# Ten transposes taken from the matrix engine: 32x32 blocks on VectorE, and a trip through HBM between partitions

## The chip, the cores and the metric

The kernel runs on one core of a Trainium2 chip. The metric is device time in microseconds; 446.53 us is the median of three runs before the change. The core's engines run side by side, each with its own queue of instructions in a fixed order: TensorE (PE, matrix products and the transposes), VectorE (DVE), ScalarE (ACT), GpSimd (POOL) and SyncE (SP, which here only issues weight transfers).

## What is computed

Two decoder layers over 256 tokens of width 1024. What matters here is the first layer, in which four retention heads and eight latent-attention heads (worked as four pairs) run from one input projection into one output projection:

```python
h = x @ w_in
rq, rk, rv, rg, mq, mkv, mkr, mg = _split(h, EVEN_SPLITS)
q_r = retnet_rotate(_heads(rq, RET_HEADS), pos)
k_r = retnet_rotate(_heads(rk, RET_HEADS), pos)
o_r = head_group_norm(retention_chunkwise(q_r, k_r, _heads(rv, RET_HEADS)))
ret_out = (_merge(o_r) * jax.nn.silu(rg.astype(jnp.float32))).astype(x.dtype)
...
o_m = causal_attention(q_full, k_full, v_m, (MLA_NOPE + MLA_ROPE) ** -0.5)   # softmax over keys, times v
mla_out = (_merge(o_m) * jax.nn.silu(mg)).astype(x.dtype)
return jnp.concatenate([ret_out, mla_out], axis=-1) @ w_out
...
x = layer_norm(DN_ALPHA * x + y, ln_g[i], ln_b[i])
```

The second layer (`moba_layer`, 16 heads of causal attention with rotary q and k, gate and output projection) is not touched.

## The kernel before

Every fp32 product is made of three float32r products (`mm3`, L174 to L176): each operand is split into a high part (ACT, L179) and a remainder (DVE, L180). So each weight tile `raw` that SP fetches becomes `w_h` on ACT and `w_l` on DVE, in six buffers each (`WBUFS`), and PE works through them unit by unit; a unit is one 512 KB weight tile. Within a head or pair the projections are units named by their PSUM tiles: `pq`/`pkk` (queries and keys of a retention head), `pv`, `pg` (values, gate), `pmg`, `pn`, `pvv` (gate, the two up-projections of a pair).

PE's order is written out by hand. Between the units, `tick()` lets waiting generators go one step; the tables at the head of the file say how many units each step waits. `retention` adds `scores` (PSUM tile `pst`, then `sd` and its split `sT`), `values` (`po`, normalised into `ro`; POOL computes the reciprocal root `rstd`) and `merge` (`ro` times the gate, then `transposed`). `mla` adds `attend` (scores `sc`, `softmax` into `prob`, `prob_T`, then the product `pom`). The order on DVE, ACT and POOL is set by the scheduler, once, when the program is built: each engine takes its instructions in that order, and one that waits holds up those behind it.

Two places transpose on PE. `transposed` turns the gated head output `ro` (two token halves of 128x512) into the layout that the output projection needs, in eight 128x128 transposes per head, and splits what lands in PSUM into `rT_h`, `rT_l`. `prob_T` turns the six 128x128 blocks of a pair's probabilities into `pT_h`, `pT_l`. The eight transposes of the rotary queries `qr` (`rotary_queries`) share two buffers, tag `ro`, with the head outputs.

Of the kernel before, what the change touches and what calls it, by code (L numbers as in the profile page):

```python
# [9 lines left out]
F32 = mybir.dt.float32  # L10
F32R = mybir.dt.float32r
# [6 lines left out]
P = 128  # L18
S = 256
NT = S // P  # L20
# [11 lines left out]
WBUFS = 6  # L32
TAIL = 5
HOLD = 5
SCO = 6, 4, 5, 8
CPT = 3, 3, 4, 5
MRG = 1, 2, 2, 6
CSC = 3, 3, 3, 3
CAV = 4, 4, 4, 1
MSC = 2, 2, 2, 2  # L40
MPT = 5, 4, 3, 3
MAV = 3, 1, 3, 3
VAL = 1, 2, 1, 1
LAT1, LAT2, QR = 5, 2, 7
WARM = 8
BY_DVE = 1
CSK = 6
DECK = 7

OFF = np.cumsum([0, 1024, 1024, 2048, 2048, 256, 256, 64, 1024])  # L50
# [107 lines left out]
def trunk(ctx, tc, x, lng, lnb, w, cst, dec, out):  # L158
    nc = tc.nc
    cp = ctx.enter_context(tc.tile_pool(name="const", bufs=1))  # L160
    wp = ctx.enter_context(tc.tile_pool(name="weights", bufs=1))
    even = ctx.enter_context(ExitStack())
    wk = even.enter_context(tc.tile_pool(name="even", bufs=1))
    ps = ctx.enter_context(tc.tile_pool(name="psum", bufs=1, space=bass.MemoryType.PSUM))
# [194 lines left out]
    def transposed(srcs, n, hi, lo):  # L359

        for d in range(0, n, 2):
# [4 lines left out]
                    nc.tensor.transpose(pv[:, k, t * P:(t + 1) * P], srcs[t][:, (d + k) * P:(d + k + 1) * P], ident)  # L366
            split_to(hi[:, d:d + 2, :], lo[:, d:d + 2, :], pv)

    lat = []
    got_qpe = []  # L370

# [91 lines left out]
    def retention(h, mid=None):  # L463

        pq, pkk = pp("pq"), pp("pkk")
        v4 = [z.rearrange("p (c s) -> p c s", c=2) for z in (pq, pkk)]
        for _ in range(KD // 2):
            ks, wv = load("qk")
            for i, k in enumerate(ks):
                for c in range(4):  # L470
                    mm3(v4[c // 2][:, c % 2, :], wv, x_rows(k), lambda z: z[:, i, c * P:(c + 1) * P],
                        lambda z: z, start=k == 0 and c % 2 == 0, stop=k == KD - 1)
            tick()
        qkT = []
        both = [wk.tile([P, 4, S], F32R, name="rqk_" + e, tag="rqk_" + e) for e in "hl"]
        for n, p in enumerate(v4):
            a = wk.tile([P, 2, S], F32, name="rot_a", tag="rot_a")
            b = wk.tile([P, 2, S], F32, name="rot_b", tag="rot_b")
            nc.vector.tensor_tensor(a, p, cosr[:, None, :].to_broadcast([P, 2, S]), op=OP.mult)
            nc.vector.tensor_tensor(b, p, sinr, op=OP.mult)  # L480
            nc.vector.tensor_tensor(a, a, b[:, ::-1, :], op=OP.add)
            qkT.append([z[:, 2 * n:2 * n + 2, :] for z in both])
            split_to(*qkT[n], a)
        qT, kT = qkT
        got = {}

        def scores():
            pst = at("pst")
            for c in range(2):
                mm3(pst[:, :S], kT, qT, lambda z: z[:, c, :P], lambda z: z[:, c, :], start=c == 0, stop=c == 1)  # L490
            for c in range(2):
                mm3(pst[:, S:S + P], kT, qT, lambda z: z[:, c, P:], lambda z: z[:, c, P:], stop=c == 1)
            sd = wk.tile([P, S + P], F32, name="sd", tag="sd")
            nc.vector.tensor_tensor(sd[:, :S], pst[:, :S], decay[:, h, :], op=OP.mult)
            nc.vector.tensor_tensor(sd[:, S:], pst[:, S:S + P], decay[:, h, :P], op=OP.mult)
            got["sT"] = split(sd, [P, S + P], "sT")
            yield 1

        def values():
            while "v" not in got or "sT" not in got:  # L500
                yield 0
            sT, v = got["sT"], got["v"]
            po = [at("po") for t in range(NT)]
            mm3(po[0], sT, v[0], lambda z: z[:, :P], lambda z: z, start=True, stop=True)
            mm3(po[1], sT, v[0], lambda z: z[:, P:S], lambda z: z, start=True)
            mm3(po[1], sT, v[1], lambda z: z[:, S:], lambda z: z, stop=True)
            got["o"] = []
            for t in range(NT):
                st = wk.tile([P, 6], F32, name="st", tag="st", bufs=2)
                nc.vector.bn_stats(st, po[t])  # L510
                r = rstd_of(st, LN_EPS, True)
                o = wk.tile([P, RDV], F32, name="ro", tag="ro", bufs=2)
                state["late"] = nc.scalar.activation(o, po[t], AF.Identity, scale=r[:, 0:1], bias=r[:, 1:2])
                got["o"].append(o)
            yield 1

        def merge():
            while "o" not in got:
                yield 0
            for t in range(NT):  # L520
                nc.vector.tensor_tensor(got["o"][t], got["o"][t], got["g"][t], op=OP.mult)
            yield MRG[h]
            hi = wk.tile([P, 4, S], F32R, name=f"rT{h}_h", tag="rT_h", bufs=2)
            lo = wk.tile([P, 4, S], F32R, name=f"rT{h}_l", tag="rT_l", bufs=2)
            transposed(got["o"], 4, hi, lo)
            for i in range(4):
                catT[4 * h + i] = (hi[:, i, :], lo[:, i, :])
            yield 1

        add(scores(), SCO[h])  # L530
        if mid:
            mid(h)
        pvv = [pp("pv") for t in range(NT)]
        block_proj("v", x_rows, pvv)
        vh = wk.tile([P, NT, RDV], F32R, name="rv_h", tag="rv_h")
        vl = wk.tile([P, NT, RDV], F32R, name="rv_l", tag="rv_l")
        for t in range(NT):
            split_to(vh[:, t, :], vl[:, t, :], pvv[t])
        got["v"] = [(vh[:, t, :], vl[:, t, :]) for t in range(NT)]
        add(values(), VAL[h])  # L540
        pg = [pp("pg") for t in range(NT)]
        block_proj("g", x_rows, pg)
        got["g"] = [gate(pg[t], [P, RDV], "rgate", 2) for t in range(NT)]
        add(merge())
# [40 lines left out]
    def prob_T(prob, j, tag, bufs):  # L585

        pt = at("ppt")
        for b in range(3):
            nc.tensor.transpose(pt[:, b * P:(b + 1) * P], prob[:, j, b * P:(b + 1) * P], ident)
        return split(pt[:, :3 * P], [P, 3 * P], tag, bufs=bufs)  # L590

    def av(o, pT, v, cols, start):

# [28 lines left out]
    def mla(p):  # L622
# [32 lines left out]
        def attend():  # L655
            while not got_qpe:
                yield 0
            sc = [at("sc") for a in range(2)]
            for a in range(2):
                causal_scores(sc[a], [z[:, a, :] for z in qn], [z[:, a, :] for z in kn])  # L660
            paired_scores(sc, [z[:, p, :] for z in qpe], kpe, False)
            prob = softmax(sc, (MN + MR) ** -0.5, "msm", 1)
            yield MPT[p]
            pTs = [prob_T(prob, a, "pT", 2) for a in range(2)]
            yield MAV[p]
            po = at("pom")
            pov = po.rearrange("p (a s) -> p a s", a=2)
            for a in range(2):
                av(pov[:, a, :], pTs[a], v, slice(a * P, (a + 1) * P), start=a == 0)
            og = wk.tile([P, 2, S], F32, name="mog", tag="og")  # L670
            nc.vector.tensor_tensor(og, pov, sg.rearrange("p (a s) -> p a s", a=2), op=OP.mult)
            hi, lo = split(og, [P, 2, S], f"mT{p}", tag="mT", bufs=2)
            for i in range(2):
                catT[16 + 2 * p + i] = (hi[:, i, :], lo[:, i, :])
            yield 1
# [163 lines left out]
    def attend_odd(q, qT, kT, v, got):  # L839

        st = {}

        def first():
            sc = [at("sc") for a in range(4)]
            quad_scores(sc, qT, kT)
            for d in range(2):
                st[d] = softmax(sc[2 * d:2 * d + 2], CD ** -0.5, "csm", 2)

        def second():
            for d in range(2):  # L850
                st[d] = [prob_T(st[d], a, "pT", 4) for a in range(2)]

        def third():
            for d in range(2):
                po = at("poc")
                pov = po.rearrange("p (a s) -> p a s", a=2)
                for a in range(2):
                    c = (q % 2) * S + d * P + a * CD
                    av(pov[:CD, a, :], st[d][a], v, slice(c, c + CD), start=a == 0)
                og = wk.tile([P, S], F32, name="cog", tag="og", bufs=2)  # L860
                for a in range(2):
                    rs = slice(a * CD, (a + 1) * CD)
                    nc.vector.tensor_tensor(og[rs, :], pov[:CD, a, :], got["g"][rs, d * S:(d + 1) * S], op=OP.mult)
                oT[2 * q + d] = split(og, [P, S], f"oT{2 * q + d}")

        first()
        yield CPT[q]
        second()
        yield CAV[q]
        while "g" not in got:  # L870
            yield 0
        third()
        yield 1
# [109 lines left out]
```

## Time and profile before

| | |
|---|---|
| median of 3 runs (446.32 to 446.73) | 446.53 us |
| profiled execution | 446.2 us |
| its span, first to last instruction | 444.4 us |
| busy: PE / DVE / ACT / POOL | 435.2 / 330.1 / 247.7 / 9.8 us |
| granted TensorE clock, mean | 0.995 |

The profiled execution stands 0.3 us under the median; 1.8 us of it lie outside the span. Busy times of several engines overlap, so they don't add up to the span; what counts is which engine the last chain of work runs through.

### The profile page before, as it was taken

Reading aid. Unit: us, or ns where it says so; the run is one execution under the profiler, and the core shown is the slowest. Engines: PE = TensorE matmul, PEld = TensorE weight load, DVE = VectorE, ACT = ScalarE, POOL = GpSimd, SP = SyncE. Lnnn points to the kernel's source line nnn. Section 1 sums busy time; section 2 is a strip of 40 time slices with the busy share of each in tenths; the row PEclk is TensorE's granted clock in tenths of the full one; section 3 lists DMA queues with packets and bytes.
Section 4 is the critical chain, followed back from the end, with each engine's and each line's share of the span. In section 5 each row is a group of like instructions: output and inputs, shape, how many; then the busy total and the mean of one; then the engine's idle time right before and its main releaser. Section 6 shows DMA issues by size and latency. Waiting matters only on the chain.

```text
span 444.4 us, 7652 instructions
## 1 busy us (share of the span) xinstructions
PE 435.2 (98%) x2958; PEld 389.5 (88%) x2958; DVE 330.1 (74%) x587; ACT 247.7 (56%) x438; POOL 9.8 (2%) x18
## 2 busy tenths in 40 slices
PE   8999999999999999999999999999999999999993
PEld 6998899988998888889998888888899999999883
DVE  5899788785876865556498569668767698889747
ACT  6777466653656553345465755503645869596810
POOL 0000000000000000000000000000000000000001
PEclk9999999999999999999999999999999999999998
DMA  8977545454463466454546557812866363634002
GB/s 297 367 228 235 184 143 188 146 170 139 143 196 126 168 215 208 154 190 160 197 143 192 183 185 239 290 50 96 279 194 189 97 191 103 190 96 137 1 1 94
DMA packets 21924, 75.55 MB, mean 170 GB/s; under 512 B 2432, under 2 KB 3072, under 8 KB 21888
## 3 DMA queue, kind: packets, MB, share of 16 engines
q1 hardware_dynamic: 20304, 70.66, 49.8%
q10 hardware_dynamic: 1584, 4.41, 2.7%
q8 instruction: 23, 0.38, 0.3%
q14 instruction: 13, 0.11, 0.1%
HBM read 74.01 MB, written 1.05 MB: 169 GB/s over the span
## 4 chain that ended last, share of the span: by engine, by line
PE 94%; DVE 2%; ACT 2%; issue 1%; DVEq 0%; ACTq 0%
PE pg L174 5%; PE pg L176 5%; PE pg L175 5%; PE pj L174 4%; PE pv L174 3%; PE pj L176 3%; PE pj L175 3%; PE pv L176 3%; PE pv L175 3%; PE acc L174 3%; PE acc L175 3%; PE acc L176 3%; PE pm L307 3%; PE pa L175 3%; PE pa L176 3%; PE pa L174 2%
## 5 line engine op out<-in xcount | busy, mean ns | idle before, releaser
L180 DVE TENSOR_TENSOR w_l<-raw,w_h 128x1024 fp32r<-128x1024 f32 (+3 forms) x133 | 155.8, 1175 | 55.9 <-ACT w_h L179 55.0
L179 ACT ACTIVATE w_h<-raw 128x1024 fp32r<-128x1024 f32 (+3 forms) x133 | 135.2, 1020 | 94.1 <-PE pa L175 19.3
L174 PE MATMUL pj<-xT_hi,w_h 128*128 128x256 f32 x128 | 36.2, 283 | 0.0
L176 PE MATMUL pj<-xT_lo,w_h 128*128 128x256 f32 x128 | 35.8, 279 | 0.0
L175 PE MATMUL pj<-xT_hi,w_l 128*128 128x256 f32 x128 | 35.7, 279 | 0.0
L174 PE MATMUL pg<-w_h,xT_hi 128*128 128x512 f32 x64 | 25.8, 403 | 0.0
L174 PE MATMUL pv<-w_h,xT_hi 128*128 128x512 f32 x64 | 25.6, 400 | 0.0
L175 PE MATMUL pg<-w_h,xT_lo 128*128 128x512 f32 x64 | 25.3, 395 | 0.0
L175 PE MATMUL pv<-w_h,xT_lo 128*128 128x512 f32 x64 | 25.2, 395 | 0.0
L176 PE MATMUL pv<-w_l,xT_hi 128*128 128x512 f32 x64 | 25.2, 395 | 0.0
L176 PE MATMUL pg<-w_l,xT_hi 128*128 128x512 f32 x64 | 25.2, 394 | 0.0
L174 PEld LDWEIGHTS pj<-xT_hi,w_h 128*128 128x128 f32 x128 | 24.0, 187 | 0.4
L175 PEld LDWEIGHTS pj<-xT_hi,w_l 128*128 128x128 f32 x128 | 24.0, 188 | 0.0
L176 PEld LDWEIGHTS pj<-xT_lo,w_h 128*128 128x128 f32 x128 | 24.0, 188 | 0.0
L174 PE MATMUL pq<-xT_hi,w_h 128*128 128x256 f32 x64 | 18.3, 286 | 0.0
L174 PE MATMUL pg<-xT_hi,w_h 128*128 128x256 f32 x64 | 18.1, 283 | 0.0
L174 PE MATMUL pmg<-xT_hi,w_h 128*128 128x256 f32 x64 | 18.0, 282 | 0.0
L174 PE MATMUL pkk<-xT_hi,w_h 128*128 128x256 f32 x64 | 18.0, 281 | 0.0
L175 PE MATMUL pkk<-xT_hi,w_l 128*128 128x256 f32 x64 | 17.9, 280 | 0.0
L175 PE MATMUL pq<-xT_hi,w_l 128*128 128x256 f32 x64 | 17.9, 280 | 0.0
L175 PE MATMUL pmg<-xT_hi,w_l 128*128 128x256 f32 x64 | 17.9, 279 | 0.0
L176 PE MATMUL pmg<-xT_lo,w_h 128*128 128x256 f32 x64 | 17.9, 279 | 0.0
(304 smaller groups left out, 1222.2 us busy)
## 6 DMA issues: line engine op xcount, KB each, us to landing
raw<-w SPq DMA_DIRECT2D x125, 512.0 KB, 4.0
raw<-w SPq DMA_DIRECT2D x7, 416.0 KB, 6.7
raw<-w SPq DMA_DIRECT2D x4, 256.0 KB, 2.7
xn<-x ACTq DMA_DIRECT2D x2, 512.0 KB, 4.4
decay<-dec ACTq DMA_DIRECT2D x1, 512.0 KB, 7.8
decay_ln<-lng ACTq DMA_DIRECT2D x1, 512.0 KB, 4.5
rv_h_ln<-lnb ACTq DMA_DIRECT2D x1, 512.0 KB, 3.9
lng_ln<-lng ACTq DMA_DIRECT2D x1, 512.0 KB, 3.5
```

The source lines that it names most:

```text
L174: nc.tensor.matmul(o, ca(a[0]), cb(b[0]), start=start, stop=False, skip_group_check=True)
L175: nc.tensor.matmul(o, ca(a[1]), cb(b[0]), start=False, stop=False, skip_group_check=True)
L176: state["mm"] = nc.tensor.matmul(o, ca(a[0]), cb(b[1]), start=False, stop=stop, skip_group_check=True)
L179: done = nc.scalar.activation(hi, src, AF.Copy)
L180: nc.vector.tensor_tensor(lo, src, hi.bitcast(F32), op=OP.subtract)
L307: state["mm"] = nc.tensor.matmul(pm[t][j][:, :288], xs[a][:, t * P:(t + 1) * P], wv[b][:, i2 * 288:(i2 + 1) * 288], start=k == 0 and e == ...
```

## The change

For retention heads 0 to 2 and all four pairs, the transposes on PE go. `moved` does the same in three steps: DVE transposes all 32x32 blocks of the tile within their 32 partitions (`turn`); POOL writes the result to HBM (`far`); POOL reads it back in four transfers, one for each group of 32 partitions (`moved`), so that the blocks land on the partitions where they belong. ACT and DVE then split `moved` in SBUF where they split PSUM before. Head 3, the rotary queries, the latents and the second layer keep PE's transposes. The tables of waits get other numbers, and the buffer that GpSimd's transfers use for their descriptors is set to 4096 bytes.

```diff
-SCO = 6, 4, 5, 8
+SCO = 7, 4, 4, 8
...
-MPT = 5, 4, 3, 3
+MPT = 7, 9, 4, 7
...
+MOVE_R, MOVE_M, MOVE_C = 3, 4, 0
...
+    def moved(src, n, w):
+        m = n * P
+        z = wk.tile([P, w], F32, name="turn", tag="turn", bufs=2)[:, :m]
+        nc.vector.transpose(z.rearrange("p (j n q) -> p j n q", j=4, n=n),
+                            src.rearrange("p (n j q) -> p j n q", n=n, j=4))
+        d = wk.tile([P, w], F32, name="moved", tag="moved", bufs=2)[:, :m]
+        far = dram.tile([P, m], F32, name=f"far{m}", tag=f"far{m}", bufs=3)
+        nc.gpsimd.dma_start(far, z)
+        fv = far.rearrange("(i k) (j c) -> j k i c", i=4, j=4)
+        for j in range(4):
+            nc.gpsimd.dma_start(d[j * 32:(j + 1) * 32, :].rearrange("k (i c) -> k i c", i=4), fv[j])
+        return d.rearrange("p (i n q) -> p n i q", i=4, n=n)
...
+            if h < MOVE_R:
+                dst = [moved(got["o"][t], 4, 768) for t in range(NT)]
             yield MRG[h]
...
-            transposed(got["o"], 4, hi, lo)
+            if h < MOVE_R:
+                for t in range(NT):
+                    split_to(*[z[:, :, t * P:(t + 1) * P].rearrange("p n (i q) -> p n i q", i=4) for z in (hi, lo)], dst[t])
+            else:
+                transposed(got["o"], 4, hi, lo)
...
+            if p < MOVE_M:
+                prob = moved_T(prob)
             yield MPT[p]
-            pTs = [prob_T(prob, a, "pT", 2) for a in range(2)]
+            pTs = pair_T(prob, "pT", 2) if p < MOVE_M else [prob_T(prob, a, "pT", 2) for a in range(2)]
...
-    nc = bacc.Bacc("TRN2", target_bir_lowering=False, num_devices=1)
+    nc = bacc.Bacc("TRN2", target_bir_lowering=False, num_devices=1, dynamic_dma_scratch_size=4096)
```

What this does to the order shows at three places. On POOL, from head 0's `rstd` to head 1's, there stood before only the reciprocal roots:

```order
L457 TENSOR_TENSOR rstd_668<-rstd_668,mhalf_75 128x1
L457 TENSOR_TENSOR rstd_678<-rstd_678,mhalf_75 128x1
L457 TENSOR_TENSOR rstd_1252<-rstd_1252,mhalf_75 128x1
L457 TENSOR_TENSOR rstd_1262<-rstd_1262,mhalf_75 128x1
```

Now the transfers of head 0's two token halves (`far512`) and of pair 0 (`far768`) stand between them:

```order
L476 TENSOR_TENSOR rstd_736<-rstd_736,mhalf_77 128x1
L382 DMA far512_778<-turn_775 128x512
L382 DMA far512_787<-turn_784 128x512
L385 DMA moved_777<-far512_778 32x4x128 x4
L385 DMA moved_786<-far512_787 32x4x128 x4
L382 DMA far768_1080<-turn_1077 128x768
L385 DMA moved_1079<-far768_1080 32x4x192 x4
L476 TENSOR_TENSOR rstd_1255<-rstd_1255,mhalf_77 128x1
```

Fifteen transfers came in ahead of head 1's `rstd`, and each group of reads waits for its write to have landed. On DVE, ahead of pair 0's softmax (L558, later L583), there stood before:

```order
L180 TENSOR_TENSOR qpe_l_739<-pt_945,qpe_h_738 128x512
L180 TENSOR_TENSOR qpe_l_739<-pt_952,qpe_h_738 128x512
L180 TENSOR_TENSOR w_l_1184<-raw_1181,w_h_1183 128x1024
L558 ISA neg_1018,msm_m_1016<-sc_989,cs_88 128x128
```

and now:

```order
L183 TENSOR_TENSOR qpe_l_710<-pt_985,qpe_h_709 128x512
L540 TENSOR_TENSOR ro_730<-ro_730,rgate_673 128x512
L498 TENSOR_TENSOR rot_a_1088<-pq_887,cosr_267 128x512
L499 TENSOR_TENSOR rot_b_1089<-pq_887,sinr_268 128x512
L540 TENSOR_TENSOR ro_740<-ro_740,rgate_676 128x512
L183 TENSOR_TENSOR qpe_l_710<-pt_992,qpe_h_709 128x512
L378 STREAM_TRANSPOSE turn_775<-ro_730 128x512
L183 TENSOR_TENSOR w_l_1225<-raw_1222,w_h_1224 128x1024
L500 TENSOR_TENSOR rot_a_1088<-rot_a_1088,rot_b_1089 128x512
L378 STREAM_TRANSPOSE turn_784<-ro_740 128x512
L583 ISA neg_1058,msm_m_1056<-sc_1029,cs_90 128x128
```

Head 0's gating and its two block transposes moved in front of that softmax. On ACT, around the split of head 1's scores (`sT_h`), there stood before:

```order
L179 ACTIVATE w_h_1364<-raw_1362 128x1024
L179 ACTIVATE rv_h_1173<-pv_1084 128x512
L179 ACTIVATE pT_h_1161<-ppt_1157 128x384
L179 ACTIVATE pT_h_1169<-ppt_1165 128x384
L179 ACTIVATE w_h_1399<-raw_1397 128x512
L179 ACTIVATE sT_h_1215<-sd_1212 128x384
```

and now:

```order
L182 ACTIVATE rT0_h_949<-moved_777 128x4x128
L182 ACTIVATE rv_h_1196<-pv_1102 128x512
L182 ACTIVATE w_h_1373<-raw_1371 128x1024
L182 ACTIVATE rv_h_1196<-pv_1103 128x512
L182 ACTIVATE rT0_h_949<-moved_786 128x4x128
L182 ACTIVATE sT_h_1192<-sd_1189 128x384
L182 ACTIVATE w_h_1428<-raw_1426 128x512
L182 ACTIVATE w_h_1449<-raw_1447 128x1024
L182 ACTIVATE pT_h_1289<-moved_1079 128x384
L182 ACTIVATE pT_h_1293<-moved_1079 128x384
```

The splits of head 0's moved halves, which need POOL's transfers, now stand in front of `sT_h`, and pair 0's behind it; the splits on DVE (`rT0_l`, `sT_l`) follow in the same order.

## Rows read from the trace of the kernel before

**Rows 1.** The page: span, busy time, and the chain that ended last.
```profile
span 444.4 us, 7652 instructions
PE 435.2 (98%) x2958; PEld 389.5 (88%) x2958; DVE 330.1 (74%) x587; ACT 247.7 (56%) x438; POOL 9.8 (2%) x18
...
PE 94%; DVE 2%; ACT 2%; issue 1%; DVEq 0%; ACTq 0%
```
**Rows 2.** PE's timeline at head 0's transposes: start, length (us), operation, count.
```profile
62.30 0.28 PE L176 MATMUL pmg<-xT_lo,w_h 128*128 128x256 f32 x1
62.42 1.03 PE L366 MATMUL pt<-cs,ro 128*128 128x128 f32 x8
63.21 0.36 PE L174 MATMUL pmg<-xT_hi,w_h 128*128 128x256 f32 x1
63.41 0.28 PE L175 MATMUL pmg<-xT_hi,w_l 128*128 128x256 f32 x1
```
**Rows 3.** PE's timeline at pair 0's transposes.
```profile
96.08 0.39 PE L176 MATMUL pv<-w_l,xT_hi 128*128 128x512 f32 x1
96.31 0.82 PE L589 MATMUL ppt<-cs,prob 128*128 128x128 f32 x6
96.88 0.48 PE L174 MATMUL pg<-w_h,xT_hi 128*128 128x512 f32 x1
97.19 0.39 PE L175 MATMUL pg<-w_h,xT_lo 128*128 128x512 f32 x1
```
**Rows 4.** Busy time by stretch: PE, PEld, DVE, ACT, POOL, clock, DMA share, GB/s.
```profile
65.00:165.00 100.00, 100.00 (x656) 89.91 (x656) 75.11 (x123) 55.01 (x89) 2.09 (x4) 1.00 0.51 159
165.00:265.00 100.00, 100.00 (x615) 88.11 (x613) 64.28 (x99) 52.24 (x82) 1.04 (x2) 1.00 0.57 181
```
**Rows 5.** DVE's timeline at pair 0's softmax.
```profile
82.29 0.29 DVE L558 CUSTOM_DVE_ANT_0 neg<-sc,cs 128x128 f32<-128x128 f32 x1
...
83.41 0.08 DVE L558 DVE_READ_ACCUMULATOR2_ANT msm_m<- 128x1 f32 x1
84.60 0.69 DVE L479 TENSOR_TENSOR rot_a<-pq,cosr 128x512 f32<-128x512 f32 x1 [1.11 <-PE pq L176]
85.21 0.68 DVE L480 TENSOR_TENSOR rot_b<-pq,sinr 128x512 f32<-128x512 f32 x1
...
86.63 1.19 DVE L180 TENSOR_TENSOR w_l<-raw,w_h 128x1024 fp32r<-128x1024 f32 x1
```
**Rows 6.** PE's timeline: where stages of heads 0 and 1 begin.
```profile
18.53 0.28 PE L174 MATMUL pq<-xT_hi,w_h 128*128 128x256 f32 x1
29.84 0.40 PE L174 MATMUL pv<-w_h,xT_hi 128*128 128x512 f32 x1
79.83 0.22 PE L174 MATMUL sc<-mqk_h 128*128 128x128 f32 x1
82.18 0.38 PE L174 MATMUL pq<-xT_hi,w_h 128*128 128x256 f32 x1
99.75 0.28 PE L174 MATMUL pst<-rqk_h 128*128 128x256 f32 x1
101.09 0.45 PE L174 MATMUL pg<-w_h,xT_hi 128*128 128x512 f32 x1
103.93 0.39 PE L174 MATMUL po<-rv_h,sT_h 128*128 128x512 f32 x1
106.00 0.40 PE L174 MATMUL pg<-w_h,xT_hi 128*128 128x512 f32 x1
```
**Rows 7.** An issue on ACT; POOL's longest group; landing times of transfers.
```profile
251.95 0.33 ACTq L765 DMA_DIRECT2D decay_ln<-lng  x1
...
L750 POOL TENSOR_TENSOR lr<-lr,mhalf 128x1 f32<-128x1 f32 x4 | 3.8, 943 | 174.7 <-DVE lr L742 128.6 <-DVE lr L749 46.1
...
raw<-w SPq DMA_DIRECT2D x4, 256.0 KB, 2.7
...
out<-xn SPq DMA_DIRECT2D x2, 256.0 KB, 2.0
```

More of the change, by code (lines that the diff above doesn't have):

```diff
@@ L34 @@
 HOLD = 5
-SCO = 6, 4, 5, 8
+SCO = 7, 4, 4, 8
 CPT = 3, 3, 4, 5
-MRG = 1, 2, 2, 6
+MRG = 5, 4, 2, 6
 CSC = 3, 3, 3, 3
 CAV = 4, 4, 4, 1
-MSC = 2, 2, 2, 2
-MPT = 5, 4, 3, 3
-MAV = 3, 1, 3, 3
+MSC = 2, 5, 2, 1
+MPT = 7, 9, 4, 7
+MAV = 2, 1, 4, 2
 VAL = 1, 2, 1, 1
-LAT1, LAT2, QR = 5, 2, 7
+LAT1, LAT2, QR = 4, 7, 6
 WARM = 8
@@ L47 @@
 CSK = 6
+MOVE_R, MOVE_M, MOVE_C = 3, 4, 0
+MOVE_ACT = 4
 DECK = 7
@@ L161, in trunk @@
     wp = ctx.enter_context(tc.tile_pool(name="weights", bufs=1))
+    dram = ctx.enter_context(tc.tile_pool(name="dram", bufs=1, space=bass.MemoryType.DRAM))
     even = ctx.enter_context(ExitStack())
@@ L590, in prob_T, with moved_T, pair_T @@
         return split(pt[:, :3 * P], [P, 3 * P], tag, bufs=bufs)
+    def moved_T(prob):
+        return moved(prob.rearrange("p a c -> p (a c)"), 6, 768)
+    def pair_T(d, tag, bufs):
+        res = []
+        for a in range(2):
+            hi, lo = [wk.tile([P, 3 * P], F32R, name=tag + e, tag=tag + e, bufs=bufs) for e in ("_h", "_l")]
+            split_to(*[z.rearrange("p (n i q) -> p n i q", n=3, i=4) for z in (hi, lo)], d[:, 3 * a:3 * a + 3])
+            res.append((hi, lo))
+        return res
     def av(o, pT, v, cols, start):
@@ L847, in first @@
                 st[d] = softmax(sc[2 * d:2 * d + 2], CD ** -0.5, "csm", 2)
+                if q < MOVE_C:
+                    st[d] = moved_T(st[d])
         def second():
             for d in range(2):
-                st[d] = [prob_T(st[d], a, "pT", 4) for a in range(2)]
+                st[d] = pair_T(st[d], "pT", 4) if q < MOVE_C else [prob_T(st[d], a, "pT", 4) for a in range(2)]
         def third():
```

## The prediction

> **What bounds the kernel now.** I read the page first: PE is busy for 98% of the span, and the chain that ended last runs through PE for 94% of it [rows 1]. Next the busy times by stretch: between 65 and 265 us, where all the groups of transposes that go but one lie, PE is busy for 200 of 200 us at full granted clock, DVE for 75 of 100 and then 64 of 100 us, POOL for 2 and 1 us [rows 4]. So in this part every instruction that PE loses is time saved, as long as PE finds no new wait; the other engines have time left over. Then I read PE's timeline around two groups of transposes, for what one costs where it stands, and the starts of PE's stages, to lay the new order out in time.
>
> **What PE loses.** Head 0's eight transposes begin at 62.42; the second matmul after them begins at 63.41. Matmuls of that shape follow each other at 0.12 us (62.30 to 62.42), so without the group it would have begun at 62.54: the group costs 0.87 us [rows 2]. Pair 0's six begin at 96.31, the second matmul after them at 97.19; at 0.23 us from one to the next (96.08 to 96.31) it would have begun at 96.54: 0.65 us [rows 3]. Both give 0.11 us per transpose. Three heads and four pairs: 3 x 0.87 + 4 x 0.65 = **5.2 us**. From the profiled execution's 446.2 us that leaves 441.0; the runs' median stands 0.3 above it, so **441.3 us** if nothing else changes. The odd layer's instructions keep their order (but for a few swaps on DVE and ACT), so nothing is expected after 300 us.
>
> [...]
>
> **What is added, and its cover.**
> - DVE: six block transposes of 128x512 and four of 128x768. No row shows one. An operation on 128x512 takes 0.61 us from start to start (84.60 to 85.21), and 128x1024 about 1.2 [rows 5]; I take 0.6 and 0.9, in all 7 us in some 200, where DVE has 61 us free [rows 4]. At twice this price it is 14 us, still covered on the whole, though not at each place.
> - The splits read SBUF in place of PSUM, same shapes, same number: I take nothing, hidden under PE's work.
> - POOL: 50 transfers, 10 writes and 40 reads. No transfer from POOL is in the trace. What one holds POOL up, call it **d**, lies between 0.33 us (an issue on ACT) and 2.0 us (a store of 256 KB lands in that time; so much if POOL had to see each one through). The nearest row is POOL's own: its longest group takes 0.94 us for 128x1 elements [rows 7]. I take d = 1.0. For landing I take 2.7 us for a write and 2.0 for a read [rows 7]; 3 MB out and 3 MB back beside 75 MB of weights change little. [...]
>
> **Where it could wait.** By the new order some 24 us of PE's work or more lie between each pair's scores and its product, and head outputs are needed almost 60 us after their gate or later. The narrow place is around head 1, where head 0's and pair 0's transfers queue up on POOL. I lay it out from t = 0, the start of the rotary queries' transposes, which now come one unit before pair 0's scores.
>
> PE: eight transposes 0.87 [rows 2]; a q/k unit 2.83 (four from 18.53 to 29.84); scores from 3.7, for 2.35 (79.83 to 82.18); four v units of 12 x 0.233 = 2.8; `pst` from 17.25, for 1.34 (99.75 to 101.09); two g units; `po` from 24.2, for 2.07; two g units and one of `pmg`; `pom` from 34.7 [rows 3, 6].
>
> DVE, in its new order, at 0.6 for 128x512 and 1.15 for a weight [rows 5]: head 0's outputs use the buffers of the rotary queries, so they can be written only after these transposes; I put the first gated half at 3.7. Then two rotations, the second half, a split and the first block transpose, done at 6.7; one weight, one rotation, the second transpose, done at 9.1. The softmax (1.1, from 82.29 to 83.41) starts 3 us after its scores. Its normalised result is turned by 18.8.
>
> - *Head 1's keys.* Their last split on DVE stands behind a weight tile that can be split on ACT only when PE has left the third v unit, at 14.5. With 1.1 on ACT and 1.1 on DVE it is done at 17.7; `pst` needs it at 17.4. **Cost 0.4 us**; 0 if I placed DVE too late, 1.5 if a block transpose costs double.
> - *Head 1's `po`.* It needs `sT`, and ACT and DVE now take head 0's moved second half first. Counting back from 24.4 (second matmul) over two splits on DVE, ACT must start that half by 22.6. POOL: the first write starts at 6.7, has landed at 9.5 + d, and eight reads follow: the last has landed at 9.5 + 9d + 2 = 20.5 with d = 1. Cost nothing, 2 us to spare; from d = 1.23 each further tenth costs 0.9 us.
> - *Pair 0's `pom`.* Write at 18.8, landed 22.5, four reads to 26.5, landed 28.5, two splits to 30: 4.7 us before 34.7. Cost nothing. From d = 1.4 on the write starts only after head 0's reads, and it is late too.
> - *Head 1's `rstd`* stands behind these on POOL, free at 26.5; `po` ends at 26.3. Nothing.
> - *Pairs 1 to 3* have 24 to 31 us from scores to product; softmax and turn 6, two passes over POOL and HBM 10, splits 2: nothing up to d = 2.
>
> Weights are split as soon as a buffer is free, six ahead of use at 2.8 us each, so ACT or DVE held up for a few us by a late transfer reach PE only through the tiles named above.
>
> Sum: 446.2 - 5.2 + 0.4 + 0.3 = **441.7 us**.
>
> **The rivals.**
> 1. *POOL is somewhat slower.* d between 1.3 and 1.7: the wait at `po` is 9 x (d - 1.23), 0.6 to 4.2 us, with up to 1 us at `pom`: 442.3 to 446. For it: nothing here shows what POOL needs for a transfer of 128 rows. Against: POOL is otherwise empty.
> 2. *POOL is much slower, and PE's saving turns into PE's wait.* If an issue on POOL has to wait for the DVE instruction beside it, d grows by about 0.75 (DVE's share) x 1.2 us = 0.9, to 1.9. Then `po` waits 9 x 0.67 = 6 us, and pair 0's transfers, which start at 26.6, are 2 us later still: 441.7 + 8 = 449.7 us. The sign turns at d = 1.7. For it: DVE is rarely idle there [rows 4]. [...]
> 3. *The gain is not there.* Block transposes at several times my price or splits in a worse order leave several small waits that add up to the saving: 446 to 447 us. Against: PE's wait would need six to ten late tiles, and only one place is narrow.
> [...]
>
> **How the numbers follow.** Forecast (441.0 to 442.3) 0.60, rival 1 0.17, rival 2 0.15, rival 3 0.07, rival 4 0.01. Predicted is the likeliest, 441.7. From below, 440.8 takes in no wait at all and the rounding of 48 distances; from above, the range reaches through rival 1 and 3 and a part of 2, to 447.5. The forecast's own range is 441.0 to 442.5. A measurement of this kernel tells about 0.2% (0.9 us) from no change. Faster by more than that (below 445.6): the forecast, rival 1 but for its end, 0.01 of rival 4: 0.76. Slower (above 447.4): most of rival 2: 0.15. Same: 0.09.
>
> **What would show it.** No `pt<-cs,ro` but head 3's and no `ppt` before 300 us; PE busy without a gap from 65 to 265 us, a span shorter by about 5 us, and 24 us between a pair's scores and its product without a wait. Distances between POOL's issues give d directly: about 1 us for the forecast, 1.3 or more for rival 1, near 2 for rival 2. A wait of `po` on `sT`, with ACT's `rT0_h<-moved` idle before it for a DMA, is rivals 1 and 2; a wait of `pst` on `rqk_l` of more than 0.5 us means DVE's block transposes are dearer than I took. The prediction is wrong if POOL's reads are not issued one behind the other at that pace, or if PE waits at a place that I did not lay out.

## The result and the profile after

The changed kernel takes 442.81 us (median of 4 runs, 442.13 to 443.51), the kernel before 446.42 (446.26 to 446.73; four runs; 446.53 was the median of the first three): a ratio of 0.9918, 95% interval 0.9907 to 0.9930. The forecast was 441.7. The measured median lies 0.3 us above the forecast's own range of 441.0 to 442.5, where the prediction had put rival 1, and inside its whole range of 440.8 to 447.5.

The page of the changed kernel, for comparison with [rows 1] and [rows 7]: span, busy times, the chain that ended last, and the new transfers (KB each, us from issue to landing).

```profile
span 440.5 us, 7684 instructions
PE 429.6 (98%) x2910; PEld 383.2 (87%) x2910; DVE 336.0 (76%) x597; ACT 247.5 (56%) x438; POOL 39.2 (9%) x68
...
PE 90%; DVE 4%; ACT 2%; DMA 1%; issue 1%; SPq 0%; DVEq 0%; ACTq 0%
...
far<-turn POOLq DMA_DIRECT2D x6, 256.0 KB, 3.9
moved<-far POOLq DMA_DIRECT2D x24, 64.0 KB, 3.9
far<-turn POOLq DMA_DIRECT2D x4, 384.0 KB, 2.9
moved<-far POOLq DMA_DIRECT2D x16, 96.0 KB, 4.7
```

PE has 48 matmuls less (2958 to 2910), POOL 50 instructions more, and the span is 3.9 us shorter, not 5.2. Busy time by stretch, as in [rows 4], says that the rest isn't in the first of the two stretches:

```profile
65.00:165.00 100.00, 100.00 (x637) 89.11 (x637) 80.63 (x134) 59.18 (x95) 20.89 (x36) 1.00 0.65 209
165.00:265.00 100.00, 99.38 (x610) 87.41 (x609) 69.46 (x105) 53.47 (x83) 12.42 (x22) 1.00 0.65 202
```

PE is idle for 0.62 us between 165 and 265. The list of PE's waits (us in total, times, longest) names what it waited for:

```profile
PE pidle L254 <- DVE mhalf L250: 1.2, 1, 1.2
PE pm L310 <- ACT w_h L182: 1.0, 2, 0.6
PE ppt L614 <- DVE pT_l L183: 0.9, 1, 0.9
PE pv L177 <- DVE mqk_l L183: 0.6, 1, 0.6
```

`pidle` and `ppt` (the second layer's) are as long in the kernel before. New are `pm`, in the input stage (below), and `pv`. PE's timeline shows head 3's second value tile begin 1.01 us after the matmul ahead of it, where 0.23 is usual (229.80 to 230.03 just before): 0.78 us lost.

```profile
18.93 0.28 PE L177 MATMUL pq<-xT_hi,w_h 128*128 128x256 f32 x1
...
230.27 0.39 PE L179 MATMUL pv<-w_l,xT_hi 128*128 128x512 f32 x1
231.28 0.50 PE L177 MATMUL pv<-w_h,xT_hi 128*128 128x512 f32 x1 [0.62 <-DVE mqk_l L183]
```

That tile needs the PSUM buffer that pair 3's keys (`pn`) held, and DVE's timeline shows why the buffer came late:

```profile
228.81 0.68 DVE L183 TENSOR_TENSOR mqk_l<-pn,mqk_h 128x512 fp32r<-128x512 f32 x1
229.41 1.21 DVE L183 TENSOR_TENSOR w_l<-raw,w_h 128x1024 fp32r<-128x1024 f32 x1
230.54 0.68 DVE L183 TENSOR_TENSOR mqk_l<-pn,mqk_h 128x512 fp32r<-128x512 f32 x1
```

The split of a weight tile that PE uses only at 247.04 stands between the splits of the pair's queries and keys.

The first row of that PE timeline is the other half of the difference. The first `pq` begins at 18.93, in [rows 6] at 18.53: 0.4 us were lost in the input stage, where the engines run the same instructions in the same order as before. So the span's account is -5.2 (48 transposes) + 0.8 (`pv`) + 0.4 (start) = -4.0, against -3.9 measured: **the price of 0.11 us per transpose holds to within 0.1 us of the span.**

The new operations, in the views of tiles `turn` and `moved` (ns: shortest, median, longest; the last row is us from issue to landing, for the reads alone):

```profile
L382 POOL DMA_DIRECT2D far<-turn x10: 553/563/736, 85.4 to 242.8; - x10
L378 DVE STREAM_TRANSPOSE turn<-ro x6: 698/702/703, 84.4 to 166.9; 128x512 f32<-128x512 f32 x6
L378 DVE STREAM_TRANSPOSE turn<-prob x4: 967/978/979, 95.9 to 241.6; 128x768 f32<-128x768 f32 x4
...
L385 POOL DMA_DIRECT2D moved<-far x40: 551/552/571, 88.3 to 248.3; - x40
...
DMA to landing us min/median/max: 2.2/4.3/7.0
```

### The profile page after: what moved, and what is told of

It reads as the page before. It is cut to its first block, busy times and chain, and to the rows that moved or that the text cites. A ratio compares the mean times of both kernels' runs of the same rounds, so it can differ in the third digit from the quotient of the medians.

```text
span 440.5 us, 7684 instructions
## 1 busy us (share of the span) xinstructions
PE 429.6 (98%) x2910; PEld 383.2 (87%) x2910; DVE 336.0 (76%) x597; ACT 247.5 (56%) x438; POOL 39.2 (9%) x68
## 4 chain that ended last, share of the span: by engine, by line
PE 90%; DVE 4%; ACT 2%; DMA 1%; issue 1%; SPq 0%; DVEq 0%; ACTq 0%
PE pg L177 5%; PE pg L179 5%; PE pg L178 5%; PE pj L177 4%; PE pv L177 4%; PE pj L179 3%; PE pj L178 3%; PE pv L179 3%; PE pv L178 3%; PE acc L177 3%; PE acc L178 3%; PE acc L179 3%; PE pa L178 3%; PE pa L177 3%; PE pa L179 3%; PE pm L310 2%
## 5 line engine op out<-in xcount | busy, mean ns | idle before, releaser
L385 POOL DMA_DIRECT2D moved<-far x40 | 21.9, 554 | 23.6 <-DMA far<-turn 6.5
L788 POOL TENSOR_TENSOR lr<-lr,mhalf 128x1 f32<-128x1 f32 x4 | 3.8, 945 | 176.2 <-DVE lr L780 128.6
L177 PE MATMUL pg<-xT_hi,w_h 128*128 128x256 f32 x64 | 18.1, 283 | 0.0
L177 PE MATMUL pq<-xT_hi,w_h 128*128 128x256 f32 x64 | 18.1, 282 | 0.0
```

Of the source, the lines that this page charges most:

```text
L177: nc.tensor.matmul(o, ca(a[0]), cb(b[0]), start=start, stop=False, skip_group_check=True)
L385: nc.gpsimd.dma_start(d[j * 32:(j + 1) * 32, :].rearrange("k (i c) -> k i c", i=4), fv[j])
L788: nc.gpsimd.tensor_tensor(r[:, 0:1], r[:, 1:2], mhalf[:, :1], op=OP.pow)
```

## The experiments

Each was timed against the kernel before on the same chip, whose median was 446.4 to 446.6 us each time. Where PE's waits are given, they are start-to-start distances beyond the usual one of the same two shapes.

### The tables alone

```diff
-MOVE_R, MOVE_M, MOVE_C = 3, 4, 0
+MOVE_R, MOVE_M, MOVE_C = 0, 0, 0
...
-            z = wk.tile([P, MH * MR], F32, name="qr", tag="ro", bufs=2)
+            z = wk.tile([P, MH * MR], F32, name="qr", tag="qr", bufs=2)
```

> The new tables with every transpose back on PE (48 matmuls more than in the changed kernel; the rotary queries get buffers of their own, since on PE the head outputs hold theirs longer). Theory A, the saving is the 48 PE instructions at 0.11 us each and the tables only make room for the transfers: 446.4 us, at most 1 us more for waits in an order that was not made for it (446.2 to 447.4). Rival, the new order by itself takes waits off PE: below 445.5. The PE wait of the second v tile of head 3 on the split of pair 3's keys (0.78 us at 231.28 in the changed kernel) is gone if DVE's block transpose of pair 2 (0.98 us just ahead) is what causes it, and stays if the order of the tables does.

Measured: **449.32 us**, ratio 1.0065 (1.0052 to 1.0078). Neither came true: the new order with PE's transposes is slower by 2.7 us. Its list of PE's waits begins:

```profile
PE pv L177 <- DVE mqk_l L183: 1.3, 1, 1.3
PE pidle L254 <- DVE mhalf L250: 1.2, 1, 1.2
PE pom L179 <- DVE pT_l L183: 1.1, 1, 1.1
```

By distances the `pv` wait is 1.42 us and `pom`'s (pair 3) 1.26, together 2.7. So the new tables bring no gain of their own while PE transposes; they cost. And the `pv` wait comes from the order that the tables make, not from DVE's block transpose, which isn't in this kernel.

### The moves alone, in the old tables

```diff
-SCO = 7, 4, 4, 8
+SCO = 6, 4, 5, 8
...
-MPT = 7, 9, 4, 7
+MPT = 5, 4, 3, 3
```

(and `MRG`, `MSC`, `MAV`, `LAT1`, `LAT2`, `QR` likewise as before the change)

> The moves with the old tables. In the changed kernel 21.2 us pass from the first score of pair 2 (211.77) to its last split (232.97). By the old order the pairs' products follow their scores by 29.0, 17.2, 18.7 and 23.4 us. Theory A: pair 1 is about 4 to 5 us late, pair 2 about 2.5 to 3.5, pairs 0 and 3 are in time; with the 5.2 saved 446.4 - 5.2 + 7.5 = 448.7 us (446.5 to 452, more if ACT and DVE, which wait in order for the late tile, hold up weights as well). Rival, the room in the tables is not needed: 441.5 to 443.

Measured: **453.11 us**, ratio 1.0157 (1.0132 to 1.0182). The room in the tables is needed. Pair 1's product waits 3.6 us and pair 2's 2.2, a little less than expected; 2.2 more go at pair 0's scores (1.1) and at head 1's `po` (1.1), and 0.7 at the output projection (`acc`). The time lies above the expected range all the same; the largest part of what was left out stands behind pair 1's wait. PE's timeline there, and the busy times by stretch with the granted clock (third number from the end):

```profile
145.30 0.40 PE L179 MATMUL pv<-w_l,xT_hi 128*128 128x512 f32 x1
149.14 0.58 PE L177 MATMUL pom<-pT_h,mv_h 128*128 128x256 f32 x1 [3.44 <-ACT pT_h L182]
...
152.89 0.63 PE L179 MATMUL pv<-w_l,xT_hi 128*128 128x512 f32 x1
153.32 0.63 PE L177 MATMUL pv<-w_h,xT_hi 128*128 128x512 f32 x1
...
154.89 0.39 PE L178 MATMUL pv<-w_h,xT_lo 128*128 128x512 f32 x1
```

```profile
145.00:149.00 4.00, 0.70 (x3) 0.21 (x2) 2.80 (x4) 2.01 (x4) 0.56 (x2) 0.86 0.95 280
149.00:151.00 2.00, 1.86 (x8) 1.77 (x9) 1.03 (x2) 0.50 (x2) 0.00 (x0) 0.50 0.66 234
151.00:153.00 2.00, 2.00 (x9) 1.81 (x9) 0.69 (x1) 0.10 (x1) 0.00 (x0) 0.50 0.05 20
153.00:155.00 2.00, 2.00 (x7) 1.57 (x6) 0.69 (x1) 0.52 (x1) 0.00 (x0) 0.57 0.00 0
```

After 3.4 idle us the granted clock is 0.50 from 149 to 153 and 0.57 from 153 to 155, and until 154.60 the `pv` matmuls follow each other at 0.43 us in place of 0.23. The twelve of `pom` and six of `pv` take 5.46 us; at a granted clock of 1.00 they take 1.32 (113.29 to 114.61 in the changed kernel) and 1.40 (six at 0.233). So 2.7 us go behind a wait of 3.6.

### One kind of move at a time

```diff
-MOVE_R, MOVE_M, MOVE_C = 3, 4, 0
+MOVE_R, MOVE_M, MOVE_C = 3, 0, 0
```

> The three heads moved, the four pairs on PE, new tables. Theory A, the savings add up by the number of PE instructions: 446.4 - 3 x 0.87 = 443.8 us (443.2 to 444.6). Rival, one kind of move brings nearly all and the other nothing: 442.5 or less, or 446 or more.

Measured: **446.57 us**, ratio 1.0001 (0.9992 to 1.0009). Against the kernel before, the rival's number; against the tables alone, from which it differs by the three heads' 24 transposes, -2.75 us, where 2.6 was expected; 0.3 of it lies at the start, where the first `pq` begins at 18.48 in place of 18.80. Both waits of the tables alone are still there (1.42 and 1.27 us). So the heads give what they should, in tables that cost as much. From here to the changed kernel the pairs give 3.8: 2.6 by 24 transposes, 1.27 by the `pom` wait, which goes, 0.64 by the `pv` wait, which shrinks to 0.78, less about half a us at the start (18.48 to 18.93).

For the pairs alone the order had to be another one, too (with the head outputs on PE, the rotary queries' place had to go back):

```diff
-LAT1, LAT2, QR = 4, 7, 6
+LAT1, LAT2, QR = 5, 2, 7
...
-MOVE_R, MOVE_M, MOVE_C = 3, 4, 0
+MOVE_R, MOVE_M, MOVE_C = 0, 4, 0
```

> The four pairs moved, the three heads on PE, new tables but for the latent path's and the rotary queries' places, which are the old ones. Theory A: 446.4 - 4 x 0.65 = 443.8 us (443.2 to 444.8), with the wait of head 3's second v tile, 0.78 us, still in it if pair 2's block transpose causes it. Rival, one kind of move brings nearly all: 442.5 or less, or 446 or more.

Measured: **455.36 us**, ratio 1.0188 (1.0174 to 1.0203). It says little on the pairs: PE waits 4.1 us for the rotary queries, which wait for the two `ro` buffers that head 0 now holds until PE has transposed it, and 2.2 us ahead of that; by estimate some 3 us more go at a lower granted clock around and behind these waits (0.68 from 75 to 80, 0.50 from 85 to 87, 0.76 from 87 to 90). That the moved heads leave `ro` as soon as DVE has turned them is a benefit that no step of the prediction had. The `pv` wait is 0.79 as in the changed kernel.

### The wait at head 3's values

```diff
         kn = nope(ukv, kvlat, 1)
+        state["keys"] = state["lo"] if p == 3 else None
...
+            if behind and not done:
+                with tc.issue_after(behind.ins):
+                    ks, wv = load(name)
```

(`state["lo"]` is the last split on DVE; the first gate tile of head 3 is loaded with `behind` set to it)

> The changed kernel with one edit: in head 3's unit the DVE split of one weight tile (w_l at 229.41 in the trace of the changed kernel, for a tile that PE uses only at 247.04) stands behind the split of pair 3's keys (mqk_l at 230.54) instead of ahead of it; a few later rows of DVE and ACT swap places with it. Theory A: the second v tile of head 3 waits for that split alone, so its wait of 0.78 us goes: 442.8 - 0.8 = 442.0 us (441.7 to 442.4). Rival, the wait moves to the next tile that stands behind the moved split: 442.6 to 443.2.

Measured: **441.83 us**, ratio 0.9902 (0.9885 to 0.9919); the changed kernel, measured beside it a second time (below), took 443.08. The `pv` wait is gone from PE's list. One weight split in the wrong place of DVE's queue was the whole wait. One of the six executions still took 443.28, so this wait alone is not what makes the changed kernel's long ones.

### More issues on POOL

```diff
         for j in range(4):
-            nc.gpsimd.dma_start(d[j * 32:(j + 1) * 32, :].rearrange("k (i c) -> k i c", i=4), fv[j])
+            dj = d[j * 32:(j + 1) * 32, :].rearrange("k (i c) -> k i c", i=4)
+            for i in range(0, 4, 2):
+                nc.gpsimd.dma_start(dj[:, i:i + 2], fv[j][:, i:i + 2])
```

> Each read in two of half the size, 80 reads in place of 40, the same bytes. Theory A: POOL takes 0.55 us for each, so the eight reads of head 0 become sixteen and end at 97.1 in place of 92.7, pair 0's write starts there (97.13 in the changed kernel, no later), its eight reads end near 105.2, have landed near 110 and are split near 111.8; PE wants them at 113.3. The splits of the heads' halves stand a few rows later on ACT and DVE in this kernel, so head 1's sT isn't behind them. Nothing is late: 442.8 us (442.3 to 444). Rival, POOL's transfers are already at the edge, and each further issue costs PE time: 444.5 or more.

Measured: **448.39 us**, ratio 1.0045 (1.0028 to 1.0062): the rival's side, but not for its reason. POOL's timeline:

```profile
87.89 6.87 POOL L387 DMA_DIRECT2D moved<-far x13
95.42 1.58 POOL L387 DMA_DIRECT2D moved<-far x3 [0.66 <-DMA moved<-far]
97.26 0.59 POOL L382 DMA_DIRECT2D far<-turn  x1 [0.25 <-issue]
105.89 1.08 POOL L478 TENSOR_TENSOR rstd<-rstd,mhalf 128x1 f32<-128x1 f32 x2 [8.04 <-DVE rstd L477]
106.93 4.26 POOL L387 DMA_DIRECT2D moved<-far x8
```

Up to pair 0's write (97.26) all went as expected. Its reads then stand behind head 1's `rstd`, for which POOL waits 8.0 us, idle; in the changed kernel they stand ahead of it, at 100.75. The scheduler had moved them, and I had laid the time out by the changed kernel's order. The reads end at 111.2 in place of the expected 105.2, and pair 0's `pom` waits 4.3 us by distances, with a lower granted clock after it (0.82 from 117 to 119, 0.50 from 119 to 121, 0.91 from 121 to 125):

```profile
PE pom L177 <- ACT pT_h L182: 2.0, 1, 2.0
PE pom L179 <- DVE pT_l L183: 1.9, 1, 1.9
```

POOL's own time isn't at its edge; what costs is the place in its queue.

With four reads in place of each one (`range(4)`, `i:i + 1`):

> Each read in four, 160 reads. Theory A: head 0's reads take POOL 88.3 to 105.9, pair 0's write lands near 109.5, its sixteen reads end near 118.3, have landed near 123 and are split near 124.5; PE wants them at 113.3, so it waits some 11 us there, and some 2.5 us more go in a stretch at the lower clock behind the wait, if that is as in the moves with the old tables: 456 us (452 to 462). This is the prediction's rival 2 made by hand. Rival, the reads go through several queues at once and POOL's count doesn't matter: 442.5 to 444.

Measured: **460.72 us**, ratio 1.0316 (1.0297 to 1.0335), within the expected range: pair 0's `pom` waits 8.5 us, pair 2's 2.9, pair 1's 1.1, and behind the two longer ones the granted clock is 0.50 from 121 to 125 and 0.50 to 0.52 from 254 to 260. Here the expected pace held: POOL's reads for head 0 end at 104.9 (105.9 expected), pair 0's at 119.2 (118.3).

```profile
PE pom L177 <- ACT pT_h L182: 11.1, 2, 8.3
```

### The changed kernel again

> The changed kernel once more, for PE's waits in the first 10 us, which summed to 1.65 us in its profile, and to between 0.47 and 1.13 us in those of the kernel before and of the four made from it so far. Theory A, they come from when the first weight tiles land and differ from run to run: another sum here, between 0.4 and 1.3 us, and a time of 442.0 to 443.6. Rival, the change makes them: again 1.5 us or more.

Measured: **443.08 us** (441.85 to 444.42, 6 executions), ratio 0.9923 (0.9903 to 0.9943). The waits in the first 10 us sum to 1.70, the rival's side. But that sum is the wrong measure, since later weights make part of it up. By the start of the first `pq` the two profiles of the changed kernel have 18.93 and 19.16, five others with all these moves 18.41 to 18.79 (among them 18.49 and 18.57 with two and four times the reads), the kernel before 18.53, the tables alone 18.80, the changed kernel with head 3 moved as well (below) 19.20. It goes with the landing of one transfer: SP's fourth load, issued at 2.1 in every profile, landed at 8.02, 8.24 and 8.30 in the three latest of these, at 7.31 in the kernel before and between 7.17 and 7.89 in all others. The stage differs by 0.8 us between profiles. That the three latest are all of the changed order without a later edit of it may be chance; a share of the change's own isn't excluded.

The profiled execution, at 444.42, was the longest of the six, and it shows something else, on ACT and on PE:

```profile
136.36 0.63 ACT L182 ACTIVATE rT_h<-moved 128x512 fp32r<-128x512 f32 x1 [4.58 <-DMA moved<-far]
136.90 1.99 ACT L182 ACTIVATE w_h<-raw 128x1024 fp32r<-128x1024 f32 x2
...
151.98 0.52 ACT L182 ACTIVATE sT_h<-sd 128x384 fp32r<-128x384 f32 x1 [1.65 <-DVE sd L514]
```

```profile
151.30 0.39 PE L179 MATMUL pg<-w_l,xT_hi 128*128 128x512 f32 x1
152.56 0.49 PE L177 MATMUL po<-rv_h,sT_h 128*128 128x512 f32 x1 [0.87 <-ACT sT_h L182]
153.15 0.50 PE L178 MATMUL po<-rv_h,sT_l 128*128 128x512 f32 x1
```

Head 1's second moved half lands late, ACT is held up for 4.6 us (1.5 in the first profile), the weight splits behind it slip, and head 2's `po` waits for `sT`: 1.7 us with the small wait at `pst` ahead of it. PE needs that moved half only some 36 us later.

### The late half out of the way, and head 3 too

```diff
+            if p == 1:
+                with tc.issue_after(state["scaled"].ins):
+                    state.pop("half")(1)
```

(in `attend`, behind the softmax; `half(1)` splits head 1's second moved half, `state["scaled"]` is the softmax's last instruction on ACT; head 1's `merge` leaves the split to this place; with the edit of the wait at head 3's values; a few other rows of ACT and DVE change places too)

> The edit of e5 and one more: the split of head 1's second moved half, for which ACT waited 4.6 us on the landing in the second profile of the changed kernel (with PE's wait at head 2's po behind it) and 1.5 us in the first, stands behind the scaling of pair 1's softmax on ACT, some 10 us later; PE uses that tile only at 171. Theory A, that landing differs from run to run and makes the upper half of the changed kernel's times (443.1 to 444.4 beside 441.9 to 442.3): no execution above 442.3 here, median 441.6 (441.3 to 442.0). Rival, the upper times come from the waits at the start or from elsewhere: some executions at 443 or more as before, median 441.8.

Measured: **441.19 us** (441.00 to 441.58), ratio 0.9883 (0.9869 to 0.9898). Better than expected, and no execution is a long one: the spread of the four is 0.6 us, in the changed kernel's two measurements 1.4 and 2.6. ACT doesn't wait at that split any more:

```profile
142.76 1.48 ACT L603 ACTIVATE prob<-prob,msm_i 128x128 f32<-128x128 f32 x4
144.15 0.61 ACT L182 ACTIVATE rT_h<-moved 128x512 fp32r<-128x512 f32 x1
```

What is left on PE's list stands in the kernel before too, or in the input stage:

```profile
PE pidle L254 <- DVE mhalf L250: 1.2, 1, 1.2
PE pm L310 <- ACT w_h L182: 1.0, 1, 1.0
PE ppt L625 <- DVE pT_l L183: 1.0, 1, 1.0
```

Its span of 439.5 us is 4.9 under the old one: -5.2, and 0.25 at the start.

Head 3 as well, `MOVE_R = 4` in the changed kernel, and then with both edits:

> The changed kernel with head 3 moved as well: eight PE transposes less. In the changed kernel head 3's second half is gated at 265.4 and PE first uses the tile at 282.8. Theory A: turn 0.7, write 0.6 + 3.9, four reads 2.2, landing 3.9, split 1.2: ready near 278.5, no wait, 442.9 - 0.87 = 442.0 us (441.6 to 442.7, with the changed kernel's own spread around it). Rival, weight tiles that stand behind the late split on ACT and DVE reach PE late, since weights are used at 260 to 290 as fast as they land: 443.0 to 445.

Measured: **442.60 us** (441.59 to 444.69), ratio 0.9923 (0.9902 to 0.9944): no wait at head 3's tile, but the spread and the `pv` wait of the changed kernel, so that 0.87 can't be told in it. Its profiled execution, at 443.05, shows a further wait that the changed kernel's profiles don't have, 0.72 us by distances at `pkk` (123.46), behind a pair's key split:

```profile
PE pkk L177 <- DVE mqk_l L183: 0.6, 1, 0.6
```

> The edits of e5, e9 and e10 together. Theory A, they add up: 441.6 - 0.87 = 440.7 us (440.3 to 441.3). Rival, head 3's move brings nothing beside them: 441.6 or more.

Measured: **440.22 us** (439.80 to 440.49), ratio 0.9860 (0.9847 to 0.9873), 0.97 under the kernel without head 3's move (0.17 of it at the start). The spread of its four executions is 0.7 us. This is the fastest version, 2.6 us under the changed kernel.

## Why the prediction was right, and where it was off

- **What PE loses, 5.2 us.** Right. In the version without new waits the span's account closes at 5.2, and the parts that could be told apart gave about their share: 2.75 for the heads (2.6 taken), 0.97 for head 3 (0.87), both with some of it from the start. The pairs' share was never measured by itself. Rival 4 (0.01) had PE transposes worth their length, and no run shows them so: one is 0.27 us long (view of tile `pt` in the kernel before), 48 of them 13 us, and the span lost 3.9.
- **DVE's block transposes, 7 us.** 8.1 by lengths (0.70 and 0.98 us), 7.3 by distances (84.43 to 85.05, 95.86 to 96.76: 0.62 and 0.90, as taken); they lie beside PE's work as laid out.
- **d, taken as 1.0 us.** 0.55, with hardly any scatter (0.551 to 0.571 for the reads), while DVE was busy for 81 of 100 us around. So the reads did not go at the pace that the prediction named as its own sign. **That DVE didn't stretch POOL's reads here** is what decides against rival 2, whose d of 1.9 needed such a stretch: eight reads from 88.34 took 4.37 us while DVE was busy for 4.50 of 4.50 us, four from 100.75 took 2.19 while it was busy for 1.24 of 2.30, 0.55 each in both.
- **Landing, taken as 2.7 and 2.0 us.** Off the other way: medians of 3.9 for the writes of heads, 3.9 and 4.7 for the reads, 7.0 at most. The rows I took come from stretches with a lower DMA share: in the kernel before it was 0.32 to 0.33 in the 3 us from the issues of three of the four 256 KB weight tiles (at 90.97, 182.5 and 205.10, landed after 2.6 to 2.8 us) and 0.61 at the fourth (40.03, 3.5 us), and 0.50 at the last stores (441 to 444); it is 0.69 to 1.01 around the groups of reads, beside the weights. That the share alone makes the difference is not shown: of two groups of four 64 KB reads, at shares of 0.77 and 0.69, the first (from 127.60) landed in a median of 3.1 us, the second (from 148.84) in 5.0. The shortest read took 2.2.
- **The narrow place.** Counted from the rotary queries' transposes (78.39), head 0's second half was turned at 9.1 (9.1 taken), `po` began at 24.4 (24.2), `pom` at 34.9 (34.7). Head 0's reads left POOL at 14.3 instead of 18.5, and the last landed at 18.1 instead of 20.5: the long landing used up 1.8 of the 4.2 us. Pair 0's reads left at 24.6 instead of 26.5 and landed at 29.1 instead of 28.5. These are two errors against each other, and that they nearly cancel at pair 0 is luck. (By the prediction's own figures pair 0's write falls behind head 0's reads from d = 1.03 on and is late from 1.36; it gives 1.4 for both.) No wait at `po` or `pom`, as forecast.
- **0.4 us at head 1's `pst`.** Not there: the key split ended at 17.4, not at 17.7. The prediction's own steps, 14.5 and twice 1.1 and 0.6 for the split itself, make 17.3; the term was a slip of the sum.
- **Pairs 1 to 3.** Pair 2 had 27 us from scores to product and used 21; I took 18.
- **What the prediction lacked**, under its own last condition, a wait at a place that it did not lay out: 0.8 us at head 3's values in both profiles of the changed kernel, from the tables' order. It priced the tables' new numbers at nothing beyond the places it had laid out; by themselves they cost 2.7 us. This is rival 3 in small, a split in a worse order. And rivals 1 and 2 do occur in small, at head 2 and by a late landing instead of POOL's pace: the transfer that stands on ACT ahead of weights. That it makes the upper half of the changed kernel's times is shown for the one long execution that was profiled (444.42), and borne out by the eight of the two versions without it, which keep within 0.7 us each. The forecast's 441.7 less the 0.4 at `pst`, plus 0.8 and the 0.4 at the start, is 442.5. The four times lie in two pairs (442.13 and 442.28, 443.35 and 443.51), so the median of 442.8 stands between them; the upper two have no profile. By its own two signs of being wrong, the reads' pace and a wait not laid out, its layout failed in these parts; that the time came within 1.1 us is owed to the price of a transpose, which is most of the sum, and in part to luck: the 0.4 that was not there made up for half of the wait that was.
- **Rivals 1 to 3 as priced** did not happen; made by hand, a POOL that is four times as long at its reads costs 18 us more than the changed kernel. Rivals 1 and 2 had also left out the lower clock behind a long wait, which added three quarters of the wait itself in the one case worked out (2.7 us behind 3.6, at 0.50 to 0.57).

Left open: why the landing of one and the same read differs by 2 us and more between executions, and whether the change has a share in the later start.

## What to carry to other kernels

Price what an engine in the bound loses by distances between starts, not by lengths (here 0.11 us a transpose, not 0.27), and then look for the order that the change needs: here the tables alone cost 2.7 us, the moves alone 6.5, and only the two together gain. An instruction whose result is needed late, above all one that waits for a transfer, should stand in its queue behind the work that has a nearer deadline, even if it could run sooner: two such edits, a weight split on DVE and a moved half on ACT, brought 1.6 us and took most of the scatter, and with them one more move gave what it should. A wait on the bounding engine can cost more than its length: here one of 3.6 us had 2.7 us more behind it, at a granted clock of 0.50 to 0.57.

## What the runs showed of the hardware beyond that

- Waits of PE of 1.1 and 1.3 us (tables alone) left the granted clock at 1.00 (234 to 240 and 268 to 274); after 3.4 us (moves alone) it was 0.50 from 149 to 153 and 0.57 from 153 to 155.
- With the reads doubled, POOL stopped after 13 of head 0's sixteen until an earlier one had landed, 0.66 us (after 14 with the smallest ones, 0.85 us). It isn't the number in a row that decides: sixteen from 119.64 went through in 8.45 us, and 22 of the smallest ones, from 122.14, in 10.84. What decides is not shown. In the changed kernel's first profile, no wait of POOL is put down to the landing of a read.
- Halving a read from 64 to 32 KB left POOL's time for it as it was (13 in 6.87 us, 0.53 each, beside 8 in 4.37, 0.55 each), and at 16 KB it was 0.49 (14 in 6.86 us): a quarter of the bytes, nine tenths of the time.
